# Sampled attention of a hybrid decoder step: the 16 pieces of far history outermost on the partitions, the 8 samples inside

## Chip, cores and metric

The kernel runs on one core of one Trainium2 chip. The metric is the device time of one execution in microseconds (us), as the median of several runs.

## What is computed

One inference step of a two-layer decoder trunk, for 512 prompt tokens of one sequence and for 8 sampled sequences with 8 new tokens each (`x_sample`, positions 2048 to 2055). Layer 0 is FFN, attention, FFN; layer 1 is FFN, state-space mixer, FFN, all in fp32 with a layer norm behind each. What matters here is attention A of layer 0 for the samples. It has 8 heads of 64, and each new token looks back over a cache of 2048 keys and values in three dilated patterns, whose softmaxes are mixed by their log-sums:

```
DILATED_PATTERNS = ((128, 1), (512, 4), (2048, 16))
for window, dil in DILATED_PATTERNS:
    steps = jnp.arange(window // dil + 1) * dil
    idx = q_idx[:, None] - steps[None, :]
    kg = jnp.take(k_all, idx, axis=1); vg = jnp.take(v_all, idx, axis=1)
    s = jnp.einsum('bqhd,bqjhd->bhqj', q, kg) * ATTN_SCALE
    ...
```

The last 512 cached positions are touched by all patterns. Of the 1536 positions ahead of them only the third pattern takes any: token l takes those whose position is l modulo 16, so 96 per token. These are the far keys and far values. For 8 samples and 8 tokens they are 2 x 12.58 MB (keys and values) of rows of 512 floats (8 heads x 64, 2 KB).

## The kernel before

**The stages.** The program goes through FFN, attention, FFN, FFN, state-space stage and FFN in a hand-written order. Matmuls are done in three passes (high x high, low x high, high x low parts of fp32 split into two fp32r values), so each 128 x 1024 block of weights is loaded by SyncE (SP) from memory into one of four buffers `wraw` (L114), cast by ScalarE into `wh` (L138), and its remainder is formed by VectorE into `wl` (L145). The casts have to wait for free slots, and the loads for free `wraw` buffers. Inside a stage, side work comes as generators that take a step each time the main loop has issued a block of matmuls (`hook`, L379): track `lo[0]` and track `lo[1]`. Every engine then runs its own instructions in the order in which they were written down.

**The far keys** (`far_keys`, L1399). They run on track `lo[1]` while the input projection and the prompt's attention are computed. For each token l (8) and each t (6) one transfer brings 128 rows of keys into `kc` (L1407, on ScalarE's queue, three buffers): `far_rows` (L1394) takes, for each of the 8 samples, the 16 rows at positions 16 t + l + 96 k, k = 0 to 15. Sample b and piece k land on partition 16 b + k. GpSimd (POOL) multiplies `kc` with `qb` (L1425), the rotated queries of token l, of which each sample's row is copied to its 16 partitions by a transfer from `d_q` (L1415, SP, once per l). VectorE sums over the 64 elements of each head into `s_o` (L1411), one step later.

**The near part and the softmax** (`near`, L1534). One generator per sample: `far_scores` (L1527) transposes `s_o` six times on TensorE and ScalarE writes the result into `so` (L1532), whose partitions are heads and tokens and whose free dims are t, sample, piece. For sample b GpSimd copies the 96 far scores out of `so` (L1561), the softmax runs over near and far scores together, and VectorE writes the far weights back into `so` (L1574).

**The far values** (`far_values`, L1620, last phase of `lo[0]`). `so` is transposed back (L1631) into `pof` (L1633), GpSimd spreads each weight over a block row with the constant `mask` (L1615), so that one matmul sums over all 128 partitions and keeps the samples apart. 24 transfers of 128 rows of 4 KB (two tokens at once, 512 KB) go through SP into `vc` (`load_far`, L1606 to L1610), which has ten buffers. For each t and each half of the tokens, 16 matmuls per transfer (L1657) add into two accumulators: 12 groups of 32 matmuls. Behind each group two more transfers are written into SP's order. `samples` (L1697) puts these phases in a row, and `out_b_now` (L1747) runs what is left of them (`lo_drain`) before the output projection of the second half (`end_group`) may start. Until then the groups stand between blocks of 24 matmuls (256 columns) of the FFN of the first token group.

```
1609  q_farv.dma_start(x, far_rows(a["cache_a_v"], t, 2 * l, 2))
1407  q_far.dma_start(kc, far_rows(a["cache_a_k"], t, l, 1))
1657  nc.tensor.matmul(fo[l // 4][j * 32:(j + 1) * 32, l % 4 * 128:(l % 4 + 1) * 128], p_[:, c0:c0 + 32],
```

Of the kernel before, what the change touches and what calls it, by code (L numbers as in the profile page):

```python
# [11 lines left out]
F32 = mybir.dt.float32  # L12
F32R = mybir.dt.float32r
I32 = mybir.dt.int32
AF = mybir.ActivationFunctionType
OP = mybir.AluOpType
# [208 lines left out]
def build(ctx, tc, a, upto=99):  # L225
    nc = tc.nc
# [16 lines left out]
    ident = cst.tile([128, 128], F32, name="ident")  # L243
# [912 lines left out]
    def attention(in_a, in_b, out_a, out_b, ffn_a):  # L1156
# [11 lines left out]
        mask = sp.tile([128, 16], F32, name="mask")  # L1168
# [225 lines left out]
        def far_rows(c, t, l, n):  # L1394

            return bass.AP(tensor=c.tensor, offset=c.offset + (16 * t + l) * 512,
                           ap=[[2048 * 512, 8], [96 * 512, 16], [1, n * 512]])

        def far_keys():  # L1399
            todo = [(l, t) for l in range(8) for t in range(6)]  # L1400
            ks = deque()

            def load(i):
                if i < len(todo):
                    l, t = todo[i]
                    kc = kp.tile([128, 512], F32, name="kc", bufs=3)
                    q_far.dma_start(kc, far_rows(a["cache_a_k"], t, l, 1))  # L1407
                    ks.append(kc)

            def add_up(kc, l, t):  # L1410
                nc.vector.tensor_reduce(s_o[:, t, :, 0:2, l], kc.rearrange("p (j h d) -> p j h d", j=4, d=64), axis=AX.X, op=OP.add)  # L1411

            def load_q(l):
                q = kp.tile([128, 512], F32, name="qb", bufs=1)
                nc.sync.dma_start(q, d_q.rearrange("(b l) c -> b l c", l=8)[:, l].unsqueeze(1).to_broadcast([8, 16, 512]))  # L1415
                return q

            load(0)
            q = load_q(0)
            yield  # L1420
            last = None
            for i, (l, t) in enumerate(todo):
                load(i + 1)
                kc = ks.popleft()
                nc.gpsimd.tensor_tensor(kc, kc, q, op=OP.mult)  # L1425
                if t == 5 and l < 7:
                    q = load_q(l + 1)
                if last:
                    add_up(*last)
                last = kc, l, t  # L1430
                yield
            add_up(*last)
# [77 lines left out]
        def sample_tasks(sa):  # L1510
# [8 lines left out]
            blks = [sa.tile([128, 128], F32, name=f"blk{i}", bufs=1) for i in range(2)]  # L1519
            for x in blks:  # L1520
                nc.gpsimd.memset(x, 0.0)
            so = sa.tile([128, 6, 8, 16], F32, name="so", bufs=1)
            bias_w = sa.tile([128, 520], F32, name="bias_w", bufs=1)
            nc.gpsimd.dma_start(bias_w, a["c_bias_w"])
            pn = acc = None
# [1 line left out]
            def far_scores():  # L1527
                for t in range(0, 6, 3):
                    ps = bank()
                    for i in range(3):  # L1530
                        nc.tensor.transpose(ps[:, i * 128:(i + 1) * 128], s_o[:, t + i].rearrange("p j h l -> p (j h l)"), ident)
                    nc.scalar.activation(so[:, t:t + 3].rearrange("p t b k -> p (t b k)"), ps[:, :384], AF.Copy, scale=-0.125)  # L1532

            def near(b):  # L1534
                kw, bk = kws.pop(b), blks[b % 2]
                kts = []
                for j in range(4):
                    ps = bank()
                    for t in range(4):
                        nc.tensor.transpose(ps[:, t * 128:(t + 1) * 128], kw[t // 2][:, t % 2, j * 128:(j + 1) * 128], ident)  # L1540
                    kt = sa.tile([128, 512], F32, name="kt", bufs=4)
                    copy(kt, ps, P["cps"])
                    kts.append(kt)
                bv = bk.rearrange("p (j m) -> p j m", m=32)
                for h in range(2):
                    rw = slice(h * 64, (h + 1) * 64)
                    nc.gpsimd.tensor_copy(bv[rw, :, h * 8:(h + 1) * 8], q_s[rw, :, b * 8:(b + 1) * 8])
                yield
                if b == 0:
                    far_scores()  # L1550
                if b < 6:
                    kws[b + 2] = load_near("cache_a_k", b + 2, "kw")
                ps, pn_ = bank(), bank()
                for j in range(4):
                    js = slice(j * 32, (j + 1) * 32)
                    nc.tensor.matmul(ps[js], bk[:, js], kts[j], start=True, stop=True)
                for j in range(4):
                    js = slice(j * 32, (j + 1) * 32)
                    nc.tensor.matmul(pn_[js, :8], bk[:, js], k_s[:, j, b * 8:(b + 1) * 8], start=True, stop=True)
                s = sa.tile([128, 616], F32, name="srow")  # L1560
                nc.gpsimd.tensor_copy(s[:, 520:].rearrange("p (t k) -> p t k", t=6), so[:, :, b])  # L1561
                st = sa.tile([128, 4], F32, name="sst", bufs=4)
                m, den = st[:, 2:3], st[:, 3:4]
                nc.vector.tensor_reduce(st[:, 0:1], s[:, 520:], axis=AX.X, op=OP.min)
                nc.vector.tensor_tensor_reduce(s[:, 512:520], pn_[:, :8], bias_w[:, 512:], -1.0, st[:, 0:1], OP.add, OP.min, st[:, 1:2])
                nc.vector.tensor_tensor_reduce(s[:, :512], ps, bias_w[:, :512], -1.0, st[:, 1:2], OP.add, OP.min, m)
                nc.scalar.activation(s, s, AF.Exp, scale=-1.0, bias=m, accum_out=den)
                nc.vector.reciprocal(den, den)
                if P["nn"]:
                    nc.vector.tensor_scalar(s[:, :512], s[:, :512], den, None, op0=OP.mult)  # L1570
                else:
                    nc.scalar.activation(s[:, :512], s[:, :512], AF.Identity, scale=den)
                nc.vector.tensor_scalar(pn[:, b * 8:(b + 1) * 8], s[:, 512:520], den, None, op0=OP.mult)
                nc.vector.tensor_scalar(so[:, :, b], s[:, 520:].rearrange("p (t k) -> p t k", t=6), den, None, op0=OP.mult)  # L1574
                yield
                yield
                if b > 1:
                    vws[b] = load_near("cache_a_v", b, "vw")
                yield
                ps = bank()  # L1580
                for t in range(4):
                    nc.tensor.transpose(ps[:, t * 128:(t + 1) * 128], s[:, t * 128:(t + 1) * 128], ident)
                pt = sa.tile([128, 4, 128], F32, name="spt")
                copy(pt.rearrange("p t m -> p (t m)"), ps, P["cps"])
                yield
                if b == 7:
                    for i in range(6):
                        load_far(i)
                yield
                vw = vws.pop(b)  # L1590
                ps = bank()
                for t in range(4):
                    for j in range(4):
                        js = slice(j * 32, (j + 1) * 32)
                        nc.tensor.matmul(ps[js, :128], pt[:, t, js], vw[t // 2][:, t % 2, j * 128:(j + 1) * 128], start=t == 0, stop=t == 3)
                o = sa.tile([128, 128], F32, name="onear")
                copy(o, ps[:, :128])
                yield
                yield
                ps = bank()[:, :128]  # L1600
                nc.tensor.transpose(ps, o, ident)
                for h in range(2):
                    rw = slice(h * 64, (h + 1) * 64)
                    copy(acc[rw, :, b * 8:(b + 1) * 8], ps[rw].rearrange("p (j m) -> p j m", m=32)[:, :, h * 8:(h + 1) * 8])
# [15 lines left out]
            def far_values():  # L1620
                ps = bank()[:64, :128]
# [6 lines left out]
                for t in range(0, 6, 3):  # L1628
                    ps = bank()
                    for i in range(3):  # L1630
                        nc.tensor.transpose(ps[:, i * 128:(i + 1) * 128], so[:, t + i].rearrange("p b k -> p (b k)"), ident)  # L1631
                    for i in range(3):
                        nc.scalar.copy(pof[:, t + i].rearrange("p (l j h) -> p j h l", l=8, j=4),  # L1633
                                       ps[:, i * 128:(i + 1) * 128].rearrange("p (j h l) -> p j h l", j=4, l=8)[:, :, 0:2])
# [4 lines left out]
                ps = bank()  # L1639
# [30 lines left out]
                for i in range(2):  # L1670
                    ps = bank()
# [86 lines left out]
    d_q = dram.tile([64, 512], F32, name="d_q")  # L1758
# [551 lines left out]
def consts():  # L2310
# [6 lines left out]
    c, s = np.cos(ang), np.sin(ang)  # L2317
# [9 lines left out]
    i = np.arange(128)  # L2327
# [6 lines left out]
    bias_sb = logc(((d >= 0) & (d < 128)) * 1)  # L2334
    p = np.arange(128)
    mask = np.zeros((128, 16), f)
    mask[:, :8] = (p[:, None] // 16 == np.arange(8))
    mask[:64, 8:] = (p[:64, None] // 8 == np.arange(8))
    out = dict(c_ident=np.eye(128, dtype=f), c_cos=cos, c_sin=sin, c_bias_a=bias_a, c_bias_b=bias_b,
               c_bias_w=bias_w, c_bias_sb=bias_sb, c_mask=mask)  # L2340
# [33 lines left out]
```

## Time and profile before

| | |
|---|---|
| median of 3 runs | 2421.53 us (2421.32 to 2424.22) |
| profiled execution | 2413.04 us, span from first to last instruction 2410.7 us |
| TensorE (PE) busy | 2305.9 us, 96% of the span |
| VectorE, ScalarE, GpSimd busy | 1556.5, 952.3 and 324.1 us |
| granted TensorE clock, mean | 0.973 of full |
| moved by DMA | 307.03 MB, 127 GB/s over the span |

The busy shares are averages over stages with different limits, and TensorE counts as busy at whatever clock it is granted. So a stage is read by its own stretch: the busy time of each engine in it, the granted clock, the share of the time in which the 16 DMA engines were busy (their mean) and what they moved. The chain of waits follows back, from the last instruction, what each step waited for.

### The profile page before, as it was taken

The numbers are of one execution on the slowest core, as the hardware profiler recorded it, in microseconds if no ns is written. First come the engines' busy times: TensorE is split into PE (matmuls) and PEld (weight loads), VectorE is DVE, ScalarE is ACT, GpSimd is POOL, SyncE is SP. The second block draws the span as 40 slices with busy tenths as digits, with TensorE's granted clock in tenths as the row PEclk, the third lists the DMA queues.
The fourth block names the chain that finished last, engine by engine and source line by source line (L and its number), as shares of the span: only waits on it lengthen the run. The fifth ranks groups of instructions, "written<-read, shape, count | busy, mean of one in ns | idle before, by whom it ended". The sixth has DMA issues, their size and how long they took to land.

```text
span 2410.7 us, 43708 instructions
## 1 busy us (share of the span) xinstructions
PE 2305.9 (96%) x17751; PEld 2242.7 (93%) x17751; DVE 1556.5 (65%) x3138; ACT 952.3 (40%) x1689; POOL 324.1 (13%) x436
## 2 busy tenths in 40 slices
PE   8999999999989899499999999999999999999998
PEld 8999999998878888389999999999999999999997
DVE  5878776767787664167545557557755565585675
ACT  3222222335467464135433424324246534242342
POOL 2012121234432200011000100000134001000000
PEclk9999999999989999699999999999999999999999
DMA  6244455356744877635654222423345322233241
GB/s 164 76 126 122 128 140 142 110 158 181 172 137 130 234 263 215 199 113 157 175 151 139 64 78 79 123 62 108 92 151 184 93 59 71 73 88 105 71 123 40
DMA packets 450857, 307.03 MB, mean 127 GB/s; under 512 B 13960, under 2 KB 420704, under 8 KB 450656
## 3 DMA queue, kind: packets, MB, share of 16 engines
q1 hardware_dynamic: 436032, 270.75, 38.4%
q0 software_dynamic: 7808, 20.38, 3.2%
q10 hardware_dynamic: 6816, 13.11, 1.9%
q8 instruction: 140, 2.29, 0.4%
q14 instruction: 61, 0.50, 0.1%
HBM read 282.07 MB, written 22.12 MB: 126 GB/s over the span
## 4 chain that ended last, share of the span: by engine, by line
PE 77%; DVE 9%; DMA 6%; ACT 4%; issue 1%; POOL 1%; SPq 1%; ACTq 0%; DVEq 0%; POOLq 0%
PE mm L592 17%; PE mm L593 17%; PE mm L594 17%; PE mm L741 4%; PE mm L743 4%; PE mm L742 4%; PE mm L1246 3%; PE mm L585 2%; PE mm L587 2%; PE mm L589 2%; DVE wl L145 2%; DMA wraw<-in_ffn_w_gate_dram 2%; DMA wraw<-in_attn_w_out_dram 1%; DMA kc<-in_cache_a_k_dram 1%; ACT s L1326 1%
## 5 line engine op out<-in xcount | busy, mean ns | idle before, releaser
L592 PE MATMUL mm<-xh,wh 128*128 128x320 f32 (+1 forms) x1880 | 568.5, 302 | 7.1 <-ACT wh L138 5.3
L594 PE MATMUL mm<-xh,wl 128*128 128x320 f32 (+1 forms) x1880 | 562.8, 299 | 8.2 <-DVE wl L145 8.0
L593 PE MATMUL mm<-xl,wh 128*128 128x320 f32 (+1 forms) x1880 | 563.0, 299 | 0.1
L138 ACT CAST wh<-wraw 128x1024 fp32r<-128x1024 f32 (+2 forms) x440 | 437.0, 1001 | 309.0 <-PE mm L593 184.7
L145 DVE TENSOR_TENSOR wl<-wraw,wh 128x1024 fp32r<-128x1024 f32 (+2 forms) x440 | 514.0, 1177 | 61.5 <-ACT wh L138 60.3
L592 PE MATMUL mm<-hh,wh 128*128 128x320 f32 (+1 forms) x1408 | 421.6, 299 | 0.8 <-ACT y L1023 0.7
L594 PE MATMUL mm<-hh,wl 128*128 128x320 f32 (+1 forms) x1408 | 416.8, 296 | 1.7 <-DVE wl L145 1.7
L593 PE MATMUL mm<-hl,wh 128*128 128x320 f32 (+1 forms) x1408 | 416.6, 296 | 0.0
L592 PEld LDWEIGHTS mm<-xh,wh 128*128 128x128 f32 x1880 | 362.4, 193 | 11.0 <-ACT wh L138 6.1
L594 PEld LDWEIGHTS mm<-xh,wl 128*128 128x128 f32 x1880 | 362.3, 193 | 9.4 <-DVE wl L145 9.4
L593 PEld LDWEIGHTS mm<-xl,wh 128*128 128x128 f32 x1880 | 362.4, 193 | 1.9 <-DVE xl L536 1.6
L592 PEld LDWEIGHTS mm<-hh,wh 128*128 128x128 f32 x1408 | 267.0, 190 | 3.3 <-ACT y L1023 0.9
L594 PEld LDWEIGHTS mm<-hh,wl 128*128 128x128 f32 x1408 | 266.9, 190 | 2.1 <-DVE wl L145 2.1
L593 PEld LDWEIGHTS mm<-hl,wh 128*128 128x128 f32 x1408 | 267.0, 190 | 0.5
L538 POOL TENSOR_SCALAR r<-r,lnb 128x256 f32<-128x256 f32 (+1 forms) x80 | 79.6, 1010 | 873.7 <-DVE xl L536 873.7
L839 DVE TENSOR_TENSOR hf<-sg,mm 128x256 f32<-128x256 f32 (+1 forms) x128 | 57.7, 451 | 202.9 <-PE mm L594 99.9
L682 ACT CAST hh<-hf 128x256 fp32r<-128x256 f32 (+1 forms) x128 | 55.4, 433 | 305.2 <-DVE hf L839 305.2
L672 DVE TENSOR_TENSOR r<-r,mm 128x256 f32<-128x256 f32 (+1 forms) x96 | 43.3, 452 | 110.4 <-PE mm L594 110.4
L741 PE MATMUL mm<-sh,wh 128*128 128x288 f32 x384 | 113.5, 296 | 0.0
L684 DVE TENSOR_TENSOR hl<-hf,hh 128x256 fp32r<-128x256 f32 (+1 forms) x128 | 60.7, 475 | 81.5 <-ACT hh L682 81.5
L742 PE MATMUL mm<-sl,wh 128*128 128x288 f32 x384 | 113.3, 295 | 0.0
L743 PE MATMUL mm<-sh,wl 128*128 128x288 f32 x384 | 113.0, 294 | 0.0
(513 smaller groups left out, 4189.8 us busy)
## 6 DMA issues: line engine op xcount, KB each, us to landing
wraw<-in_ffn_w_gate_dram SPq DMA_DIRECT2D x110, 512.0 KB
wraw<-in_ffn_w_up_dram SPq DMA_DIRECT2D x110, 512.0 KB
wraw<-in_ffn_w_down_dram SPq DMA_DIRECT2D x80, 512.0 KB
wraw<-in_ffn_w_down_dram SPq DMA_DIRECT2D x40, 384.0 KB
wraw<-in_attn_w_in_dram SPq DMA_DIRECT2D x28, 512.0 KB
kc<-in_cache_a_k_dram ACTq DMA_DIRECT2D x48, 256.0 KB
vc<-in_cache_a_v_dram SPq DMA_DIRECT2D x24, 512.0 KB
kw<-in_cache_a_k_dram SPq DMA_DIRECT2D x16, 512.0 KB
```

Source lines behind the costliest of these rows:

```text
L138: self.nc.scalar.copy(u.h[:, :u.n], u.src)
L145: self.nc.vector.tensor_tensor(u.l[:, :u.n], u.src, u.h[:, :u.n].bitcast(F32), op=OP.subtract)
L538: nc.gpsimd.tensor_scalar(r[:, c, self.g], r[:, c, self.g], lnb[:, k:k + 1], self.scale, op0=OP.add, op1=OP.mult)
L592: nc.tensor.matmul(ps, u.h[:, ws(k)], th[:, k, g], start=k == 0, stop=False)
L593: nc.tensor.matmul(ps, u.h[:, ws(k)], tl[:, k, g], start=False, stop=False)
L594: nc.tensor.matmul(ps, u.l[:, ws(k)], th[:, k, g], start=False, stop=k == nk - 1)
L684: late_lo.append(lambda: (nc.gpsimd if P["hp"] else nc.vector).tensor_tensor(hl[:, c, t], hf, hh[:, c, t].bitcast(F32), op=OP.subtract))
L741: nc.tensor.matmul(ps, u.h[:, ws], xh_[:, k], start=k == 0, stop=False)
L742: nc.tensor.matmul(ps, u.h[:, ws], xl_[:, k], start=False, stop=False)
L743: nc.tensor.matmul(ps, u.l[:, ws], xh_[:, k], start=False, stop=k == 3)
L839: nc.vector.tensor_tensor(hf, sg, pu, op=OP.mult)
L1246: nc.tensor.matmul(ps, x, w, start=j == 0, stop=j == len(mms) - 1)
```

## The change

The 128 partitions of far keys, far values and the queries' copies are renumbered: piece k of sample b moves from partition 16 b + k to partition 8 k + b. For this the outer two dims of the transfers' access patterns are exchanged, `so` holds t, piece, sample in place of t, sample, piece, and the mask names the sample of a partition as p modulo 8 in place of p // 16.

```
 def far_rows(c, t, l, n):
     return bass.AP(tensor=c.tensor, offset=c.offset + (16 * t + l) * 512,
-                   ap=[[2048 * 512, 8], [96 * 512, 16], [1, n * 512]])
+                   ap=[[96 * 512, 16], [2048 * 512, 8], [1, n * 512]])
 ...
 def load_q(l):
-    nc.sync.dma_start(q, d_q.rearrange("(b l) c -> b l c", l=8)[:, l].unsqueeze(1).to_broadcast([8, 16, 512]))
+    nc.sync.dma_start(q, d_q.rearrange("(b l) c -> b l c", l=8)[:, l].unsqueeze(0).to_broadcast([16, 8, 512]))
 ...
-so = sa.tile([128, 6, 8, 16], F32, name="so", bufs=1)
+so = sa.tile([128, 6, 16, 8], F32, name="so", bufs=1)
 ...
-nc.scalar.activation(so[:, t:t + 3].rearrange("p t b k -> p (t b k)"), ps[:, :384], AF.Copy, scale=-0.125)
+nc.scalar.activation(so[:, t:t + 3].rearrange("p t k b -> p (t k b)"), ps[:, :384], AF.Copy, scale=-0.125)
 ...
-nc.gpsimd.tensor_copy(s[:, 520:].rearrange("p (t k) -> p t k", t=6), so[:, :, b])
+nc.gpsimd.tensor_copy(s[:, 520:].rearrange("p (t k) -> p t k", t=6), so[:, :, :, b])
 ...
-nc.vector.tensor_scalar(so[:, :, b], s[:, 520:].rearrange("p (t k) -> p t k", t=6), den, None, op0=OP.mult)
+nc.vector.tensor_scalar(so[:, :, :, b], s[:, 520:].rearrange("p (t k) -> p t k", t=6), den, None, op0=OP.mult)
 ...
-nc.tensor.transpose(ps[:, i * 128:(i + 1) * 128], so[:, t + i].rearrange("p b k -> p (b k)"), ident)
+nc.tensor.transpose(ps[:, i * 128:(i + 1) * 128], so[:, t + i].rearrange("p k b -> p (k b)"), ident)
 ...
-mask[:, :8] = (p[:, None] // 16 == np.arange(8))
+mask[:, :8] = (p[:, None] % 8 == np.arange(8))
```

The order of the instructions is the same on all five engines. The one row that reads otherwise is VectorE's write of the far weights into `so`, eight times; here it is for one sample, with `sst` the sums of the softmax and `srow` its row:

```order
 L1568 RECIPROCAL sst<-sst 128x1
 L1573 TENSOR_SCALAR pn<-srow,sst 128x8
-L1574 TENSOR_SCALAR so<-srow,sst 128x6x16
+L1574 TENSOR_SCALAR so<-srow,sst 128x96
 L145 TENSOR_TENSOR wl_10112<-wraw,wh_10111 128x1024
 L839 TENSOR_TENSOR hf<-sg,mm 128x256
```

The 96 elements, six runs of 16 before, now form one series with an even step of 8 elements. Nothing moved.

## Rows read from the trace of the kernel before

**Rows 1.** The page's chain that ended last, shares of the span by engine.
```profile
PE 77%; DVE 9%; DMA 6%; ACT 4%; issue 1%; POOL 1%; SPq 1%; ACTq 0%; DVEq 0%; POOLq 0%
```

**Rows 2.** Stretches: from:to, length, busy PE PEld DVE ACT POOL, granted clock, DMA share, GB/s.
```profile
875.00:900.00 25.00, 25.00 (x295) 22.42 (x294) 14.80 (x39) 14.42 (x25) 1.69 (x9) 1.00 0.97 329
...
950.00:990.00 40.00, 29.26 (x309) 26.19 (x311) 10.75 (x14) 9.47 (x14) 3.37 (x6) 0.83 0.74 198
990.00:1016.00 26.00, 6.45 (x112) 3.53 (x104) 0.77 (x2) 1.35 (x2) 1.12 (x2) 0.60 0.65 198
1016.00:1024.00 8.00, 2.83 (x48) 1.85 (x48) 0.00 (x0) 0.00 (x0) 0.00 (x0) 0.50 0.53 202
1024.00:1028.00 4.00, 1.49 (x24) 0.59 (x16) 0.00 (x0) 0.59 (x1) 0.00 (x0) 0.50 0.32 129
...
929.00:1034.00 105.00, 65.60 (x722) 55.62 (x722) 23.50 (x39) 19.07 (x37) 7.84 (x12) 0.75 0.64 189
```

**Rows 3.** What TensorE waited for, 925 to 1060 us: total, times, longest.
```profile
PE aux L1657 <- DMA vc<-in_cache_a_v_dram: 31.0, 14, 4.2
PE mm L592 <- ACT wh L138: 5.2, 2, 3.3
```

**Rows 4.** The chain of waits, 840 to 1080 us: start, length, what.
```profile
937.16 20.06 DMA wraw<-in_ffn_w_gate_dram
...
957.60 15.45 DMA wraw<-in_ffn_w_gate_dram
...
1013.96 14.31 DMA vc<-in_cache_a_v_dram
1028.32 1.08 PE aux L1657 x16
```

**Rows 5.** DMA from 925 to 1030 us: queue q1 is SP's; issues with KB each.
```profile
DMA packets 18548, 21.08 MB, mean 201 GB/s; under 512 B 640, under 2 KB 14956, under 8 KB 18540
...
q1 hardware_dynamic: 18540, 20.96, 66.8%
...
vc<-in_cache_a_v_dram SPq DMA_DIRECT2D x24, 512.0 KB
```

**Rows 6.** ScalarE's queue over the whole span: packets, MB, share of 16 engines.
```profile
q10 hardware_dynamic: 6816, 13.11, 1.9%
```

**Rows 7.** Stretches of the far keys, columns as in rows 2.
```profile
545.00:600.00 55.00, 53.49 (x426) 45.59 (x426) 42.29 (x132) 31.08 (x90) 23.05 (x23) 1.00 0.65 190
...
780.00:800.00 20.00, 15.91 (x140) 14.72 (x136) 11.34 (x21) 8.04 (x13) 9.07 (x11) 1.00 0.88 198
```

**Rows 8.** The chain of waits, 545 to 840 us.
```profile
554.24 6.38 DMA kc<-in_cache_a_k_dram
...
584.39 6.89 DMA kc<-in_cache_a_k_dram
...
787.76 9.30 DMA kc<-in_cache_a_k_dram
797.19 1.28 POOL kc L1425
...
800.86 5.94 DMA bk<-in_cache_b_k_dram
```

**Rows 9.** What GpSimd and TensorE waited for, 545 to 830 us.
```profile
POOL kc L1425 <- DMA kc<-in_cache_a_k_dram: 75.8, 29, 11.8
...
PE mm L594 <- DVE wl L145: 5.8, 2, 4.5
```

**Rows 10.** Issues of the loads of far and near keys: ns min/median/max.
```profile
L1407 ACTq DMA_DIRECT2D kc<-in_cache_a_k_dram x48: 602/603/1216, 550.5 to 787.8; - x48
...
L1516 SPq DMA_DIRECT2D kw<-in_cache_a_k_dram x16: 367/424/1814, 806.8 to 894.2; - x16
```

**Rows 11.** The operations on `so` with a new step: ns min/median/max.
```profile
L1574 DVE TENSOR_SCALAR so<-srow,sst x8: 263/266/268, 848.2 to 919.1; 128x96 f32<-128x96 f32 x8
...
L1561 POOL COPY srow<-so x8: 263/263/418, 843.8 to 909.9; 128x96 f32<-128x96 f32 x8
```

## Prediction

> **What bounds the kernel now.** I began with the chain that ended last: 77% of it is TensorE, but 6%, some 145 us, is waiting for transfers [rows 1]. So the next view was the busy time by stretches, looking for places where TensorE is not full, and the one that stands out is the far values. From 950 to 1028 us TensorE's busy time falls from 29.26 of 40 us to 6.45 of 26 us, and its granted clock from full to 0.50, the lower of its two levels [rows 2]. The view of waits says what for: 31.0 us on the far values `vc` at the matmuls of L1657, and 5.2 us more on freshly cast weights [rows 3]; in the chain of waits the same stretch is one transfer behind another, weights that landed 20.06 and 15.45 us after their issue, and the last `vc`, 14.31 us [rows 4].
>
> So the stretch is bound by transfers. But are they at their limit? At 875 to 900 us the 16 DMA engines were busy 0.97 of the time and moved 329 GB/s. From 1016 to 1024 us, when almost nothing but `vc` is left, TensorE waits, and yet the share is 0.53 and the rate 202 GB/s [rows 2]. A flat share of one half while somebody waits means that eight of the sixteen engines work without pause and eight stand idle. The far transfer's outermost dim has 8 entries (the samples); that is the number that fits.
>
> This reading can be tested on the sum. In the pure stretch a busy engine moves 202 / (16 x 0.53) = 23.8 GB/s [rows 2], so a row of 4 KB takes 172 ns. The 24 transfers of 128 rows [rows 5] are 3072 x 172 ns = 528 us of engine time, 66 us on each of eight engines. All transfers of SP's queue between 925 and 1030 us took 66.8% of 16 engines [rows 5], that is 105 x 16 x 0.668 = 1122 us. The rest, nearly all weights, is 594 us, or 37 us on each of sixteen. Eight engines then have 66 + 37 = 103 us of work, and the others 37. The last rows came in just before 1028 us [rows 2, 4], 103 us behind 925. So the eight loaded engines explain the length of the stretch by themselves.
>
> **The change, part by part.**
>
> *Far values.* The bytes, rows, issues and their order stay, and the outermost dim now has 16 entries. Ends: nothing is gained if the transfers stay on eight engines or if rows get twice as dear; if all sixteen share the 1122 us evenly, each has 70 us, and the last row lands at 995 in place of 1028, 33 us earlier. Could TensorE follow? It was busy 65.60 us from 929 to 1034, at a mean clock of 0.75 [rows 2]; placed behind one another these end at 995 at the same clocks, and sooner at full clock, so it ends at about the same time as the transfers. Since two limits that lie this close delay one another now and then, I take 30 us. The upper end is 40: the same 21.08 MB [rows 5] at the 329 GB/s of 875 to 900 us [rows 2] take 64 us, which is 39, and a little comes from a clock that has not fallen when the output projection starts. What is late next is TensorE's own work and the weights, which still stand in SP's order among the far values.
>
> On what the engines' number hangs, no row shows directly. The Trainium skill, page "DMA: Bandwidth & Descriptors", section "Why a DMA increments its semaphore by 16 and not by 1", says that a transfer is dealt to as many engines, at most 16, as divide the outermost sizes of both its patterns: 8 here before, 16 after. The trace agrees for the 8 (share 0.53); for the 16 of this pattern no row stands.
>
> *Far keys.* ScalarE's queue moved 6816 packets in 1.9% of 16 engines' span, 733 us, or 108 ns for one, nearly all of them the 48 x 128 rows of `kc` [rows 6]. They are 663 us of engine time, 83 us on each of eight engines during the 250 us of this stage, 41 us on each of sixteen. Transfers are not the limit of most of it: between 545 and 600 us TensorE was busy 53.49 of 55 us [rows 7], so the `kc` pieces of 6.38 to 6.89 us in the chain there [rows 8] and GpSimd's 75.8 us of waiting for `kc` [rows 9] lie mostly beside TensorE's work, and are worth 0 to 3 us. The end of the stage is different. From 780 to 800 us the DMA share is 0.88 and TensorE lacks 4 us [rows 7]; the chain goes through the last `kc` (9.30 us), its product on GpSimd and then the load of `bk` [rows 8], with a wait of TensorE of 4.5 us for `wl` [rows 9]. About five `kc` lie in these 20 us: 5 x 128 x 108 ns = 69 us, 8.6 us on eight engines, 4.3 us on sixteen. I take 4 us there and 1 us ahead of it, 5 in sum. Ends: -3 us, if the issue on ScalarE's queue, 603 ns now against 424 ns of the near keys [rows 10], should get dearer (48 of them, beside ScalarE's work except at some steps), and 12 us, if the weights of this stage, which share the eight engines, gain as well.
>
> *Queries' copies.* Eight transfers of 256 KB out of 16 KB. The same 128 rows, now on sixteen engines; between 0 and 1 us, taken as 0.
>
> *The steps inside `so`.* L1574 on VectorE and L1561 on GpSimd, eight times 266 and 263 ns [rows 11], get a step of 8 elements. Free at best; if each took twice as long it would be 4.2 us on two engines that have room in this stretch (VectorE 14.80 of 25 us, GpSimd 1.69 [rows 2]), under 1 us on the path. Taken as 0. ScalarE's write, the transposes back and the spreading with the mask keep their shapes and get none.
>
> Sum: 30 + 5 = 35 us. The profiled execution took 2413.04 us, so 2378.0 on its scale. It lies 8.5 us below the median of the runs, 2421.53; taking the 35 us from the median gives the forecast, **2386.5 us**. A difference under 0.2%, 4.8 us, cannot be told from no change.
>
> **The rivals.**
>
> *Gain in part.* Sixteen engines are kept busy but each is slower, because together they near what the memory gives. For it: in 780 to 800 us a share of 0.88 moved only 198 GB/s [rows 7]. Against it: 329 GB/s at 0.97 [rows 2]; the poor rate goes with the weights' short rows (14956 of 18548 packets under 2 KB [rows 5]), which are in my 594 us already. Midway between the two rates, at 264 GB/s, the 21.08 MB take 80 us, the stretch ends 23 us sooner, and with nothing from the keys the time is 2398.5. Chance 0.13.
>
> *It doesn't do what it says.* The number of engines hangs on something else than the outermost dim, for example on the tile, and stays 8. Then every term is 0: 2421.5 us. Against it: near keys and weights, whose outermost dim is 128, fill all sixteen (0.97 [rows 2]) into tiles of the same 128 partitions. Chance 0.05.
>
> *Slower: rows of one engine too far apart.* Each engine now reads eight rows that lie a whole sample (2048 x 2 KB = 4 MiB) apart, where it read sixteen rows 192 KB apart. If reads at that distance get in one another's way, the 528 us of far rows grow by a factor x: (528 x + 594) / 16 is 103 at x = 2.0, so up to there the sixteen engines make up for it, and beyond it the stretch gets longer. At x = 2.5 it is 120 us, 17 us more, and the keys, (663 x 2.5) / 16 = 104 in place of 83 us per engine, add some 4: 2442.5. Against it: before, eight engines read eight samples side by side, 4 MiB apart at any moment, at 23.8 GB/s each, no less than the mean of 21.2 (329 / 16 / 0.97) at 875 to 900 us [rows 2]. Chance 0.04.
>
> The same page of the Trainium skill, section "Latency and other measured facts", has a rule on this: copies with a row pitch of 4 MiB ran at 103 GB/s where 207 and 214 were had at other pitches. By that rule x would be about 2.1 and the time some 2424, no change; the trace before, with that distance between engines, does not show such a loss.
>
> **How the numbers follow.** Forecast 0.78, part 0.13, nothing 0.05, slower 0.04. Faster by over 0.2%: 0.78 + 0.13 = 0.91; within it 0.05; slower 0.04. The range: both upper ends, 40 + 12 = 52 us, give 2369.5, and the part case with the keys' lower end, 23 - 3 = 20 us, gives 2401.5; with some 3 us for the spread of the runs shown (2421.32 to 2424.22), 2367 to 2405.
>
> **What would show it.** Right: between 950 us and the end of the far values a DMA share near 0.9 and 280 GB/s or more, the wait of L1657 for `vc` below 10 us in place of 31.0, the end of the last group near 990 to 1000 us, a clock at or near full before the output projection, and `kc` in the chain near 797 us shorter than 9.30 us. Wrong: a share still near 0.5 with waits as before (the engines' number), a share near 1 at 200 GB/s (slow rows), or the waits gone and the time back in waits for weights.

## The result and the profile after

The change takes the median from 2421.43 to 2389.39 us (4 runs each, 2387.44 to 2395.31 after), a ratio of 0.9878 with a 95% interval of 0.9857 to 0.9899. The medians differ by 32.0 us; by the ratio and its interval the gain is 24.5 to 34.6 us. The forecast was 2386.5 in a range of 2367 to 2405, so time and direction came out as said. The way there did not: the far values gave little more than half of what was forecast, the far keys about twice as much.

First, did sixteen engines take part? Part 3 of the profile's page after the change: the total, then queue, packets, MB and share of 16 engines for SP's queue and ScalarE's:

```profile
DMA packets 451497, 307.04 MB, mean 128 GB/s; under 512 B 14600, under 2 KB 421344, under 8 KB 451296
...
q1 hardware_dynamic: 436288, 270.75, 39.6%
...
q10 hardware_dynamic: 7200, 13.11, 1.9%
```

ScalarE's queue has 384 packets more than before [rows 6], 8 for each of the 48 loads of `kc`, and the whole program 640 more than its 450857, 8 for each of the 80 changed transfers (24 + 48 + 8). All 640 are under 512 B (13960 before). One small packet more for each engine that joined: eight engines became sixteen. The Trainium skill, page "DMA: Bandwidth & Descriptors", section "Why a DMA increments its semaphore by 16 and not by 1", says that each engine that takes part posts one count of its own, and that the outermost sizes set their number; these counts agree with both.

Now the far values. Stretches of the changed kernel's trace, columns as in rows 2:

```profile
950.00:990.00 40.00, 24.14 (x310) 20.11 (x310) 10.23 (x15) 9.05 (x14) 4.38 (x8) 0.84 1.06 224
990.00:1016.00 26.00, 10.70 (x137) 6.41 (x137) 1.94 (x6) 1.11 (x3) 0.00 (x0) 0.52 0.82 173
1016.00:1024.00 8.00, 7.96 (x53) 7.73 (x54) 3.50 (x5) 3.89 (x5) 0.00 (x0) 1.00 0.35 101
...
1000.00:1008.00 8.00, 2.62 (x44) 1.26 (x33) 0.00 (x0) 0.00 (x0) 0.00 (x0) 0.50 1.07 234
```

The share went from 0.74 to 1.06 (it adds up the times of single packets, so above 1 packets of one engine overlap), and yet the rate only from 198 to 224 GB/s [rows 2]. While almost only `vc` was left it was 202 on eight engines and is 234 on sixteen. What TensorE waited for, 925 to 1060 us, and SP's queue from 920.7 to 1013 us, the stretch that answers to rows 5:

```profile
PE aux L1657 <- DMA vc<-in_cache_a_v_dram: 27.0, 14, 4.3
PE mm L594 <- DVE wl L145: 1.9, 2, 1.4
```

```profile
DMA packets 18745, 21.08 MB, mean 228 GB/s; under 512 B 832, under 2 KB 15153, under 8 KB 18737
...
q1 hardware_dynamic: 18737, 20.97, 101.9%
```

The same bytes took 92.3 x 16 x 1.019 = 1505 us of engine time, where the prediction carried over 1122. If the rest still took 594 us, a far row costs (1505 - 594) / 3072 = 297 ns in place of 172. The stretch from 1000 to 1008 us, read as the prediction read its own, gives the same: 234 / (16 x 1.07) = 13.7 GB/s for a busy engine, or 300 ns for a row of 4 KB. The wait for `vc` fell only from 31.0 to 27.0 us [rows 3]. The chain still goes through these transfers:

```profile
965.82 9.91 DMA wraw<-in_attn_w_out_dram
975.80 12.60 DMA wraw<-in_attn_w_out_dram
988.46 10.88 DMA vc<-in_cache_a_v_dram
999.42 12.30 DMA vc<-in_cache_a_v_dram
1011.76 1.08 PE aux L1657 x16
```

The last group of far matmuls starts at 1011.76, 16.6 us earlier than before [rows 4]; some 4 us of that had been won ahead of the stage. At the end of the far keys the last `kc` has left the chain; what is there is a load of weights and then `bk`, 5.9 us earlier than in rows 8:

```profile
786.18 7.26 DMA wraw<-in_ffn_w_gate_dram
...
794.92 6.80 DMA bk<-in_cache_b_k_dram
```

The terms taken as nothing were small. The issue of `kc` got cheaper (603 to 543 ns [rows 10]); the two operations on `so` got dearer (266 to 316 and 263 to 352 ns [rows 11]), 1.1 us in all. From the transposes of `bk` (L1452) to that of `pn` (L1622), where both lie, the trace before has 133.4 us and the one after 134.2:

```profile
L1407 ACTq DMA_DIRECT2D kc<-in_cache_a_k_dram x48: 543/543/655, 552.9 to 784.3; - x48
...
L1574 DVE TENSOR_SCALAR so<-srow,sst x8: 309/316/333, 844.0 to 914.9; 128x96 f32<-128x96 f32 x8
...
L1561 POOL COPY srow<-so x8: 349/352/513, 839.5 to 905.7; 128x96 f32<-128x96 f32 x8
```

The profiled execution after took 2395.31 us, the slowest of its four runs, while that of before was below all of its runs (2413.04). So the spans of the two traces, 2410.7 and 2392.9 us, differ by 17.8 us, less than the medians, and gains read off against the trace before come out rather small.

### The profile page after: what moved, and what is told of

Its sections match the earlier page's. It is cut to its first block, busy times and chain, and to the rows that moved or that the text cites. A ratio compares the mean times of both kernels' runs of the same rounds, so it can differ in the third digit from the quotient of the medians.

```text
span 2392.9 us, 43708 instructions
## 1 busy us (share of the span) xinstructions
PE 2298.4 (96%) x17751; PEld 2236.0 (93%) x17751; DVE 1555.2 (65%) x3138; ACT 952.9 (40%) x1689; POOL 320.0 (13%) x436
## 2 busy tenths in 40 slices
DMA packets 451497, 307.04 MB, mean 128 GB/s; under 512 B 14600, under 2 KB 421344, under 8 KB 451296
## 4 chain that ended last, share of the span: by engine, by line
PE 80%; DVE 9%; DMA 4%; ACT 4%; issue 1%; SPq 1%; POOL 1%; ACTq 0%; DVEq 0%; POOLq 0%
PE mm L592 17%; PE mm L593 17%; PE mm L594 17%; PE mm L1246 4%; PE mm L741 4%; PE mm L743 4%; PE mm L742 4%; PE mm L585 2%; PE mm L587 2%; PE mm L589 2%; DVE wl L145 2%; DMA wraw<-in_ffn_w_gate_dram 1%; DMA vc<-in_cache_a_v_dram 1%; DMA wraw<-in_attn_w_out_dram 1%; DVE xl L536 1%
## 5 line engine op out<-in xcount | busy, mean ns | idle before, releaser
L538 POOL TENSOR_SCALAR r<-r,lnb 128x256 f32<-128x256 f32 (+1 forms) x80 | 74.3, 943 | 871.6 <-DVE xl L536 871.6
```

Source lines behind the costliest of these rows:

```text
L538: nc.gpsimd.tensor_scalar(r[:, c, self.g], r[:, c, self.g], lnb[:, k:k + 1], self.scale, op0=OP.add, op1=OP.mult)
```

## The experiments

Each was timed beside the kernel before, on the same chip. Where an expectation says that other rows are summed, the kernel is a measure and not one to use. Two stretches of each trace tell the parts apart: "keys" is from the first matmul of the input projection (L1246) to the transposes of `bk` (L1452), "far" from the transpose of `pn` (L1622) to the last far matmul (L1657), by the start times of these rows. GB/s is the rate from 950 to 975 us. Behind "far" all traces have 1379 to 1383 us.

| run | ratio to before (95%) | keys us | far us | GB/s |
|---|---|---|---|---|
| before | 1 | 337.0 | 88.7 | 203 |
| changed kernel | 0.9878 (0.9857 to 0.9899) | 333.1 | 76.3 | 227 |
| `after_again` | 0.9884 (0.9862 to 0.9905) | 332.4 | 74.4 | 227 |
| `values_only` | 0.9933 (0.9918 to 0.9949) | 338.8 | 73.1 | 240 |
| `keys_only` | 0.9964 (0.9952 to 0.9976) | 331.0 | 89.8 | 208 |
| `values_pitch_2040` | 0.9885 (0.9869 to 0.9901) | 329.9 | 70.3 | 228 |
| `values_k98` | 0.9885 (0.9857 to 0.9912) | 331.8 | 75.0 | 228 |
| `values_k98_b2046` | 0.9882 (0.9854 to 0.9909) | 331.4 | 71.9 | 234 |
| `pieces_16_rows` | 0.9889 (0.9859 to 0.9918) | 333.5 | 78.9 | 219 |
| `before_k98` | 0.999 (0.9971 to 1.001) | 340.6 | 91.3 | 210 |
| `engine_contiguous` | 0.989 (0.9875 to 0.9905) | 329.9 | 74.1 | 236 |
| `rows_8kb` | 0.9929 (0.9914 to 0.9944) | 331.0 | 81.8 | 217 |
| `values_contiguous` | 0.9807 (0.979 to 0.9823) | 330.0 | 53.6 | 287 |
| `values_own_blocks` | 0.9801 (0.977 to 0.9833) | 333.1 | 51.5 | 293 |

### The parts apart

`values_only`: the change, but

```
-ap=[[96 * 512, 16], [2048 * 512, 8], [1, n * 512]])
+ap=[[96 * 512, 16], [2048 * 512, 8], [1, n * 512]] if n == 2 else [[2048 * 512, 8], [96 * 512, 16], [1, n * 512]])
-... .unsqueeze(0).to_broadcast([16, 8, 512])
+... .unsqueeze(1).to_broadcast([8, 16, 512])
```

> Only the far values take the new partitions; far keys and the queries' copies keep the samples outermost, and ScalarE's write into `so` exchanges piece and sample. Theory A (the gain comes from the far values, whose transfers go from eight to sixteen engines): 25 to 30 us of the 32 us of the full change. Theory B (most of the gain comes from the far keys and the weights beside them, while the far values win little, since their rows became dearer): under 15 us. In the profile, by both: a DMA share near 1 from 950 us on; by B no more than about 225 GB/s there and 25 us or more of waiting for `vc` at L1657.

`keys_only`: the kernel before, with the opposite choice in both places, and ScalarE's write into `so` exchanged here too.

> Only the far keys and the queries' copies take the new partitions; far values as before. Theory A: 3 to 8 us faster than before, `vc` wait at L1657 as before (31 us). Theory B: 17 us or more. With the run of the values alone it also shows whether the two parts add up to 32 us.

`after_again`: the changed kernel.

> The changed kernel once more, on the chip of the other three runs, as their measure. Its ratio to before should be 0.986 to 0.990; its profile should again show a DMA share near 1 with about 220 GB/s during the far values.

Against a median of 2417.20 us of before, the values alone win 17.5 us (2399.66; by the interval 12.3 to 19.8), the keys and queries 9.7 (2407.52), together 27.2; the full change wins 27.8 (2389.41). The parts add up. Theory A wanted 25 to 30 from the values and 3 to 8 from the keys, theory B under 15 and over 17: both are missed, and the values still give the larger part. What holds of B is that the rows became dearer: the share is 1.02, at 240 GB/s and with 24.3 us of waiting for `vc`, just beyond the bounds that B had named (225 GB/s at most, 25 us or more). The eleven traces with the new keys have 329.9 to 333.5 us in the stretch "keys", the three with the old ones 337.0 to 340.6. In the keys' run the last `kc` stays in the chain, and takes 5.66 in place of 9.30 us [rows 8]:

```profile
783.34 5.66 DMA kc<-in_cache_a_k_dram
789.13 1.30 POOL kc L1425
...
792.83 6.25 DMA bk<-in_cache_b_k_dram
```

### Is it the distance of the rows?

`values_pitch_2040` puts the samples of the far values 2040 rows apart, `values_k98` the pieces 98 rows, `values_k98_b2046` both (98 and 2046); `before_k98` does to the kernel before what `values_k98` does to the changed one. The edit of the first:

```
-ap=[[96 * 512, 16], [2048 * 512, 8], [1, n * 512]])
+ap=[[96 * 512, 16], [(2048 if n == 1 else 2040) * 512, 8], [1, n * 512]])
```

> The full change, but the far values of neighbouring samples are read 2040 rows apart in place of 2048 (4 MiB less 16 KB), so for samples 1 to 7 other rows of the same cache are summed; engines, number and length of rows, bytes and order stay. Theory P (rows of one engine 4 MiB apart get in one another's way): a row costs about 172 ns again, the share falls below 1 with 280 GB/s or more, the wait of L1657 for `vc` falls from 27 us to under 12 us and the time falls by a further 10 to 20 us. Theory M (sixteen engines together meet a limit of the memory or of the writing side, wherever the rows lie): within 3 us of the full change and 210 to 225 GB/s as there.

> The full change, but neighbouring pieces of the far values lie 98 rows apart in place of 96 (192 KB plus 4 KB), so other rows of the same cache are summed; engines, lengths, bytes and order stay. Theory L (all 128 rows of one transfer start at the same offset modulo 64 KB, since 96 rows are 3 x 64 KB and a sample is 4 MiB, and reads that share these address bits share a part of the memory): the rows now start at sixteen different offsets, the rate during the far values rises from about 220 to 280 GB/s or more, the wait of L1657 for `vc` falls from 25 us to under 12 us, and the time falls by 8 to 20 us against the full change. Theory M (a limit of sixteen engines together that does not hang on addresses): within 3 us of the full change.

> As the run with 98 rows between pieces, and the samples 2046 rows apart in place of 2048, so that the rows of one engine do not share their low address bits either. Theory L in the form that only rows read by different engines at one time get in one another's way: within 3 us of the run with 98 rows alone. If the rows of one engine count too: a further 3 us or more. Theory M: within 3 us of the full change.

> The kernel before (eight engines), with neighbouring pieces of the far values 98 rows apart in place of 96; other rows of the same cache are summed. Both theories: eight engines were each at their own pace (23.8 GB/s), so within 3 us of before and a DMA share of about 0.53 while only `vc` is left. A gain of 8 us or more would say that the addresses held back the eight engines too.

`pieces_16_rows` keeps the set of positions and deals them out otherwise:

```
-offset=c.offset + (16 * t + l) * 512, ap=[[96 * 512, 16], [2048 * 512, 8], [1, n * 512]])
+offset=c.offset + (256 * t + l) * 512, ap=[[16 * 512, 16], [2048 * 512, 8], [1, n * 512]])
```

> The full change with the 96 far positions of a token dealt out in another way: transfer t takes positions 256 t + l + 16 k, so neighbouring pieces lie 16 rows (32 KB) apart in place of 96, for keys and values alike; the sum is over the same positions, and the result the same. Theory L: two offsets modulo 64 KB in place of one, so a part of the gain of the run with 98 rows, 3 to 12 us against the full change. Theory M: within 3 us.

All five lie with their siblings: 0.9882 to 0.9889 for the changed kernel's, 0.999 for that of before. The stretch "far" moves by up to 4.5 us either way from the 74.4 us of `after_again`, but the times don't. Theories P and L, which asked for a further 8 us or more, fall (a few us would not show in these intervals): no rule on equal low address bits or on a pitch of 4 MiB carries the loss.

### Is it that they are scattered?

`values_contiguous` reads the 128 rows of a transfer one behind another, `engine_contiguous` only the eight of one engine, and `values_own_blocks` is the former with a piece of its own for each transfer:

```
+values_contiguous:  [[8 * 1024, 16], [1024, 8], [1, n * 512]]
+engine_contiguous:  [[96 * 512, 16], [1024, 8], [1, n * 512]]
+values_own_blocks:  as values_contiguous, offset of transfer i (i // 3 * 2048 + i % 3 * 256) * 512
```

> The full change, but the 128 rows of one transfer of far values follow one another in memory (512 KB in one piece, of the first sample), as those of the near keys do; other rows of the same cache are summed. Sixteen engines, rows of 4 KB, bytes and order stay. Theory S (scattered rows: the memory delivers rows that lie far apart at some 220 to 250 GB/s in all, whatever their low address bits): 280 GB/s or more during the far values, the wait of L1657 for `vc` under 12 us, 8 to 20 us faster than the full change. Theory W (the limit is on the writing side or in the mixture with the weights' short rows): within 3 us of the full change, 210 to 250 GB/s as there.

> The full change, but the eight rows of one engine follow one another in memory (32 KB), and the sixteen engines lie 192 KB apart; other rows of the same cache are summed. Theory S, in the form that it is the eight rows of one engine that must lie near: the same gain as with all rows in one piece. Theory S, in the form that all engines must read near one another: most of the loss stays, within 4 us of the full change. Theory W: within 3 us.

> As the run with the 128 rows of a transfer in one piece, but each of the 24 transfers reads a piece of 512 KB of its own (three in each sample), where the pieces of that run overlapped, so that 12.58 MB of different rows are read as in the full change; other rows of the same cache are summed than there. Theory S (it is the scatter of the rows over the memory that costs): the same gain, 15 to 22 us against the full change (some 0.980 of before), 280 GB/s or more. Theory R (the gain of that run came from reading the same rows again and again): within 4 us of the full change (0.987 to 0.990), 210 to 250 GB/s.

Here the stretch gives way. With each transfer in a piece of its own (`values_own_blocks`) the time is 0.9801 of before, 2369.41 against 2417.59 us, or 48.2 us. The stretches of `values_own_blocks` and its wait for `vc`:

```profile
930.00:950.00 20.00, 20.00 (x234) 18.89 (x233) 11.72 (x21) 8.36 (x19) 3.36 (x4) 1.00 1.06 365
950.00:975.00 25.00, 21.94 (x331) 19.97 (x328) 7.08 (x10) 7.01 (x10) 4.49 (x8) 1.00 1.10 293
975.00:985.00 10.00, 4.10 (x64) 2.45 (x64) 0.00 (x0) 0.00 (x0) 0.00 (x0) 0.50 1.08 320
```

```profile
PE aux L1657 <- DMA vc<-in_cache_a_v_dram: 9.3, 7, 2.6
```

Engines, number and length of rows, bytes and order are those of the full change (451497 packets in both); only the places differ. At 975 to 985 us, with the weights mostly through, sixteen engines get 320 GB/s from rows in one piece. The changed kernel run again gets, from its scattered ones, late in its own stage:

```profile
985.00:995.00 10.00, 2.16 (x32) 1.25 (x32) 0.00 (x0) 0.00 (x0) 1.12 (x2) 0.50 1.09 219
995.00:1003.00 8.00, 2.16 (x32) 1.20 (x32) 0.00 (x0) 0.00 (x0) 0.00 (x0) 0.50 1.11 228
```

The engine time says the same. SP's queue in `values_contiguous` from 917 to 984 us, nearly the bytes of rows 5:

```profile
q1 hardware_dynamic: 18727, 20.91, 105.5%
```

That is 67 x 16 x 1.055 = 1131 us, where the prediction carried over 1122. With the same 594 us for the rest, a row costs 175 ns: in one piece and on sixteen engines about what it cost scattered on eight.

So it is the scatter that costs, as theory S says, and R falls (own pieces win as much as overlapping ones, 0.9801 and 0.9807). W falls too: the writing side and the weights beside it were the same. That the eight rows of one engine lie together is not enough (`engine_contiguous`, 0.989).

`rows_8kb` makes twelve transfers of 1 MB with rows of 8 KB out of the 24:

```
-x = sa.tile([128, 2, 512], ...); q_farv.dma_start(x, far_rows(a["cache_a_v"], t, 2 * l, 2))
+x = sa.tile([128, 4, 512], ...); q_farv.dma_start(x, far_rows(a["cache_a_v"], t, 4 * l, 4))
```

> The full change with four tokens per transfer of far values: twelve transfers of 1 MB with rows of 8 KB into five buffers twice as large (near keys and values and the small cache share these buffers in the same bytes as before); the result stays the same. Theory S: half as many places to go to, so a part of the gain, 3 to 10 us against the full change. Theory W: within 3 us.

Meant as an improvement, it was 11 us slower than the changed kernel's times (2400.48 against 2389.4), where theory S had expected 3 to 10 us of gain. Its rate was not higher (217 GB/s), so longer rows did not help, and the wait for `vc` rose to 31.3 us. Larger portions, each waited for as a whole, may be why; that was not tested.

## Why the prediction was right, and where it was not

**What bounds the stretch.** Right. Eight of sixteen engines had the far rows, the outermost size sets the number, and the change brings all sixteen in (packet counts, share 1.06).

**Far values: 30 us forecast, 17.5 measured** (interval 12.3 to 19.8). The step that failed is "if all sixteen share the 1122 us evenly": it took the 172 ns of a row as fixed. It became 297 ns, since scattered rows come at some 220 to 235 GB/s in all, and eight engines had already drawn 202. With the rows in one piece the step held: 1131 us of engine time, 67 us on each of sixteen engines, and a stretch "far" of 53.6 in place of 88.7 us, 35 us less where the text had 33. For the scattered rows the right sum was a limit on the rate: 202 to 234 while `vc` is alone is a gain of 14% of the 89 us of the stretch, some 12 us; the traces show 12 to 16. The text named this case among the rivals, "sixteen engines are kept busy but each is slower", gave it 0.13, and set its rate at 264 GB/s; in the far values it is what came true. What spoke against it, 329 GB/s at 875 to 900 us, was a stretch of near keys, near values and weights, and the near rows lie in one piece: it told nothing of scattered rows. The forecast that the wait would fall under 10 us and the rate reach 280 failed with it, and so did the end of the last group (1012.8 us, not 990 to 1000) and the clock near full (0.52 from 990 to 1016 us). What TensorE waits for is still `vc`. The sign that the text had set for slow rows, a share near 1 at 200 GB/s, is close to what the trace shows (1.06 at 224).

**Far keys: 5 us forecast, 9.7 measured** (0.9964, interval 5.8 to 11.6 us), inside the bounds of -3 to 12. The 4 us at the end of the stage came as worked out: the last `kc` went from 9.30 to 5.66 us. The 1 us ahead of it was too little: the stretch "keys" is 6.0 us shorter in the trace of the keys alone, and it takes 331.6 us in the mean of the eleven traces with the new keys and 338.8 in that of the other three, 7.2 us, so some 3 us came ahead of the end. The weights of this stage, which shared the eight engines, are the likely giver, but no run separates them.

**Queries' copies, steps inside `so`, the issue.** As said, nothing that can be seen.

**The rivals.** "Slower" asked for rows that cost over twice as much; they cost 1.7 times. And its mechanism is not the one at work: not the 4 MiB between the rows of one engine (`values_pitch_2040` and `engine_contiguous` change nothing), but the scatter of the whole transfer. The Trainium skill, page "DMA: Bandwidth & Descriptors", section "Latency and other measured facts", puts copies with such a pitch at about half rate and mends them by padding; here a pitch 16 KB short of 4 MiB left 0.9885, so no run here shows that rule.

**The sum** of 35 us against 27.8 and 32.0 came out right by luck: the two errors, -12 and +5, partly made up for one another. The stretch was not understood.

## What to carry to other kernels

A DMA share stuck near one half while an engine waits points to a transfer that is dealt to half the engines; look at its outermost dim. But engine time is not a constant to be shared out: before dividing it by more engines, look in the trace for a stretch in which more engines read the same pattern of addresses, and if there is none, keep the rate that is already drawn as one bound. A rate measured on rows in one piece is no bound for rows that are scattered.

## What the runs showed that was not expected

Scattered rows of 4 KB came at 202 GB/s with eight engines and 219 to 234 with sixteen; the same number of rows in one piece of 512 KB at 320, each with some of the weights among them. Neither breaking up equal low address bits, nor laying one engine's eight rows together, nor rows of 8 KB changed that. What it is in a scattered transfer that holds it back, and how near the engines must read to one another, stays open; rows in one piece on eight engines were not tried either.
